# A planned two-layer transformer kernel: a port that one engine holds, loads in source order, and work that gets its engine in the plan

## The chip, the core and the metric

The program runs on one core of one Trainium2 chip. The core's engines each take their instructions in program order: TensorE (PE; its weight loads are shown apart as PEld), VectorE (DVE), ScalarE (ACT), GpSimd (POOL) and SyncE (SP), whose queue issues all DMA transfers here. The metric is the device time of one execution in microseconds, the median of several runs.

## The reference, cut to what matters

```python
for i in range(DEPTH):                      # DEPTH 2
    mod_lat = silu(c) @ ada_w[i] + ada_b[i] # six vectors: shift, scale, gate, twice
    mod_ctx = silu(c_ctx) @ ada_w[i] + ada_b[i]
    u_lat = modulate(rms_norm(h_lat, g_mix[i]), sh1, sc1)      # 512 x 1024
    u_ctx = modulate(rms_norm(h_ctx, g_mix[i]), csh1, csc1)    # 256 x 1024
    if i == 0:   # 16 heads of 64; q, k normed per head; 8 x 16 neighbourhood plus all context, with a bias table
        y_lat = neighborhood_attention(ql, kl, vl, kc, vc, na_rpb) @ na_wo
        y_ctx = context_attention(qc, kc, vc) @ na_wo
    else:        # 16 query heads, 4 key heads, rotary; window of 128 plus all context, sink logits
        y_lat = sliding_window_attention(ql, kl, vl, kc, vc, sink) @ swa_wo
    h_lat = h_lat + ga1 * y_lat
    h_lat = h_lat + ga2 * (relu(modulate(rms_norm(h_lat, g_mlp[i]), sh2, sc2) @ w1) ** 2 @ w2)   # width 4096
    # in layer 0 the same for h_ctx
return h_lat
```

Everything is fp32. The kernel keeps that precision by splitting an operand x into a high part H (a cast on ACT to a format that TensorE reads fast) and a low part L = x - H (a subtraction), and by three products H·H, H·L and L·H.

## The kernel before, in words

The program has two layers, each with an attention and an MLP; in the order of time: the opening, the first attention (16 heads in 8 pairs), its output product, the first MLP, the second attention, its output product, the second MLP.

*The opening.* `ada01(q)`, q from 0 to 3, multiplies a quarter of the columns for the first layer's shift and scale with the conditioning vector (tile `s`): eight loads of `ada_w` each; `mods01(q)` transposes the result. `stats` sums squares of the input (`xT`, later `cT`); `mod0` makes from both the operands of the first products; `load0(p, units)` loads and splits a unit of `wqkv` for head pair p; `qkv0(0)` makes the 144 products (128 x 384) of pair 0. `bias_tables` copies 32 pieces of the position bias inside DRAM (tiles `bias_i`, `bias_e`); the heads load them from there.

*The attentions.* For each token tile `front` copies the product from PSUM, norms per head (`head_norm`, small operations on the tile `smalls`) and writes the result twice (`dup_mult`); `back` transposes it. `attn0` and `Head1` make scores, subtract the maximum, take Exp on ACT with its sum, a reciprocal on DVE, and normalise P with it, then transpose P (in layer 0 the first with the matrix `perm`) and multiply by V. In the layer-1 head, P has four tiles, two of 512 columns and two of 640.

*The MLPs.* `Stream` loads 128 x 1024 weight tiles and splits each (`split`); `relu2` makes the squared ReLU with one more subtraction `hL`. Beside the first MLP runs `ada(1, ...)`, the six vectors of layer 1 (48 tiles of `ada_w`): scalings on ACT and POOL and two additions of 128 x 1024 for nearly every tile on POOL.

*What sets the order.* Nothing is issued as the code runs. Each call makes a `Step` with an engine, and `Plan` records what it reads and writes. `Plan.search` then draws up an order for each engine: `forward` is a list scheduler which walks through time with a cost for every step (`cost`), takes the step of lowest rank that is ready, and models a port shared by DVE and POOL: a step with `port` waits until the port is free. The ranks come from latest start times (`latest`) and from gaps of TensorE (`hurry`), 40 rounds, the best one is kept. So all instructions carry the line of the call that issues them, L432. The engine of a step is written in the code, by `v`, `s`, `g`, `pe`, `sy`; for instance the subtraction in `split` is on `v` unless a caller asks for `g`.

## Time and profile before

| what | value |
|---|---|
| median of 3 runs | 1662.59 us (1661.06 to 1669.87) |
| the profiled execution, own time | 1661.9 us |
| its span, first to last instruction | 1660.1 us |
| TensorE busy | 1601.2 us, 96% |
| VectorE, ScalarE, GpSimd busy | 1136.5, 808.7, 553.9 us |
| moved by DMA | 165.63 MB, 100 GB/s over the span |
| mean granted TensorE clock | 0.992 of full speed |

Busy times are of the whole span; the stages differ, and the rows below are by stage. Idle time of an engine costs nothing unless TensorE or the last instruction waits for it. `FA`, `RA` and `R` are large SBUF tiles, each holding many things; `pq` are the eight PSUM banks.

### The profile page before, as it was taken

The numbers are of one execution on the slowest core, as the hardware profiler recorded it, in microseconds if no ns is written. First come the engines' busy times: TensorE is split into PE (matmuls) and PEld (weight loads), VectorE is DVE, ScalarE is ACT, GpSimd is POOL, SyncE is SP. The second block draws the span as 40 slices with busy tenths as digits, with TensorE's granted clock in tenths as the row PEclk, the third lists the DMA queues.
The fourth block names the chain that finished last, engine by engine and source line by source line (L and its number), as shares of the span: only waits on it lengthen the run. The fifth ranks groups of instructions, "written<-read, shape, count | busy, mean of one in ns | idle before, by whom it ended". The sixth has DMA issues, their size and how long they took to land.

```text
span 1660.1 us, 25159 instructions
## 1 busy us (share of the span) xinstructions
PE 1601.2 (96%) x9554; PEld 1357.5 (82%) x9554; DVE 1136.5 (68%) x2178; ACT 808.7 (49%) x1668; POOL 553.9 (33%) x371
## 2 busy tenths in 40 slices
PE   4999999999989999999999999999999899999999
PEld 3878888987778888888888888797767888888887
DVE  4787666778458656675666666899996766655654
ACT  4587666778435334344352433658874522332320
POOL 1121111122247419485682652475631400000000
PEclk9999999999999999999999999999999899999999
DMA  9723443114314334334342332010114232233301
GB/s 295 213 74 102 134 150 121 47 42 126 103 63 128 97 101 132 103 114 127 115 140 76 115 106 73 32 58 14 46 45 146 89 102 90 89 101 102 102 26 52
DMA packets 63802, 165.63 MB, mean 100 GB/s; under 512 B 6848, under 2 KB 24640, under 8 KB 63552
## 3 DMA queue, kind: packets, MB, share of 16 engines
q1 hardware_dynamic: 63680, 164.02, 31.2%
q8 instruction: 75, 1.23, 0.3%
q14 instruction: 47, 0.39, 0.1%
HBM read 159.79 MB, written 7.34 MB: 101 GB/s over the span
## 4 chain that ended last, share of the span: by engine, by line
PE 80%; DVE 8%; ACT 5%; issue 3%; DMA 3%; POOL 1%; SPq 0%; POOLq 0%; DVEq 0%; ACTq 0%
PE pq L432 80%; DVE FA L432 3%; DVE RA L432 2%; ACT RA L432 2%; DVE smalls L432 1%; DMA FA<-in_ada_w_dram 1%; ACT FA L432 1%; ACT R L432 1%; DMA FA<-in_wqkv_dram 1%; POOL FA L432 0%; DVE R L432 0%; ACT smalls L432 0%; DMA R<-in_ada_w_dram 0%; SPq L432 0%; DMA FA<-in_wo_dram 0%
## 5 line engine op out<-in xcount | busy, mean ns | idle before, releaser
L432 PE MATMUL pq<-RA 128*128 128x512 f32 (+3 forms) x6784 | 1268.5, 342 | 13.1 <-DVE RA L432 5.4
L432 PEld LDWEIGHTS pq<-RA 128*128 128x128 f32 x6784 | 1083.1, 190 | 166.8 <-issue 16.6
L432 ACT CAST RA<-FA 128x1024 fp32r<-128x1024 f32 (+3 forms) x283 | 224.9, 812 | 370.7 <-PE pq L432 256.5
L432 DVE TENSOR_TENSOR RA<-FA,RA 128x1024 fp32r<-128x1024 f32 (+3 forms) x249 | 297.5, 1209 | 113.6 <-ACT RA L432 109.9
L432 DVE SCALAR_TENSOR_TENSOR FA<-pq,mods,FA 128x512 f32<-128x512 f32 (+1 forms) x413 | 266.0, 662 | 138.6 <-PE pq L432 137.4
L432 POOL TENSOR_TENSOR R<-R,FA 128x1024 f32<-128x1024 f32 x84 | 218.2, 2628 | 6.7 <-ACT FA L432 4.6
L432 POOL TENSOR_TENSOR FA<-FA,smalls 128x512 f32<-128x512 f32 (+1 forms) x108 | 95.9, 892 | 322.5 <-DVE smalls L432 250.4
L432 PE MATMUL pq<-RA,R 128*128 128x512 f32 (+1 forms) x870 | 177.6, 353 | 3.4 <-DVE RA L432 3.4
L432 PEld LDWEIGHTS pq<-RA,R 128*128 128x128 f32 x870 | 144.4, 191 | 27.6 <-DVE RA L432 3.8
L432 POOL TENSOR_SCALAR FA<-FA,s 128x1024 f32<-128x1024 f32 x24 | 77.5, 3230 | 180.8 <-DMA FA<-in_ada_w_dram 166.0
L432 PE MATMUL pq<-ident,FA 128*128 128x128 f32 x802 | 124.1, 276 | 9.4 <-DVE FA L432 2.5
L432 PEld LDWEIGHTS pq<-ident,FA 128*128 128x128 f32 x802 | 92.0, 140 | 30.4 <-issue 9.4
L432 POOL TENSOR_TENSOR FA<-FA 128x256 f32<-128x256 f32 (+2 forms) x97 | 75.2, 791 | 120.2 <-ACT FA L432 109.4
L432 POOL TENSOR_TENSOR RA<-FA,RA 128x1024 fp32r<-128x1024 f32 (+2 forms) x34 | 72.4, 2140 | 128.5 <-ACT RA L432 96.4
L432 ACT COPY R<-pq 128x512 f32<-128x512 f32 (+3 forms) x200 | 89.6, 477 | 37.6 <-PE pq L432 36.4
L432 ACT ACTIVATE FA<-FA,smalls 128x512 f32<-128x512 f32 (+1 forms) x120 | 89.1, 743 | 25.4 <-DVE smalls L432 25.0
L432 ACT COPY FA<-pq 128x256 f32<-128x256 f32 (+4 forms) x130 | 56.1, 432 | 87.5 <-PE pq L432 80.1
L432 ACT ACTIVATE FA<-FA,s 128x1024 f32<-128x1024 f32 x60 | 69.1, 1151 | 60.1 <-POOL FA L432 50.8
L432 DVE SCALAR_TENSOR_TENSOR FA<-pq,FA 128x512 f32<-128x512 f32 (+1 forms) x96 | 57.1, 596 | 53.5 <-ACT FA L432 53.4
L432 ACT ACTIVATE FA<-pq 128x512 f32<-128x512 f32 (+1 forms) x96 | 49.9, 522 | 73.0 <-PE pq L432 71.9
L432 ACT ACTIVATE FA<-FA 128x256 f32<-128x256 f32 (+1 forms) x131 | 59.0, 457 | 49.5 <-DVE FA L432 38.3
L432 PE MATMUL pq<-R 128*64 128x512 f32 (+2 forms) x448 | 78.9, 463 | 0.0
(77 smaller groups left out, 979.1 us busy)
## 6 DMA issues: line engine op xcount, KB each, us to landing
FA<-in_w_dram SPq DMA_DIRECT2D x128, 512.0 KB, 3.5
FA<-in_ada_w_dram SPq DMA_DIRECT2D x80, 512.0 KB, 3.9
FA<-in_wqkv_dram SPq DMA_DIRECT2D x32, 384.0 KB, 3.7
FA<-in_wo_dram SPq DMA_DIRECT2D x16, 512.0 KB, 3.5
FA<-in_ada_w_dram SPq DMA_DIRECT2D x20, 256.0 KB, 5.9
FA<-in_wq_dram SPq DMA_DIRECT2D x8, 512.0 KB, 3.6
R<-in_ada_w_dram SPq DMA_DIRECT2D x12, 256.0 KB, 6.3
FA<-in_xT_dram SPq DMA_DIRECT2D x4, 512.0 KB, 7.7
```

What stands on the lines that cost most here:

```text
L432: tc.keep_in_program_order(getattr(e, f)(*map(real, args), **{k: real(x) for k, x in kw.items()}))
```

## The change

It has three parts. First, the model of the shared port: a step waits for it only where the other engine holds it, the holder keeps it to the end of its step, a DVE step may begin 138 ns earlier, and POOL doesn't choose a step with `port` while DVE holds the port. Second, the loads made by `load` up to the end of the opening (`strict`) are chained: each may be planned only after the load ahead of it in the source has been issued. Third, a step may have several forms, one for each engine that can do it: `gv` for POOL or DVE, `sv` for ACT or DVE, and `scaled` (the normalisation of P) for all three. `forward` puts such a step on the lists of all its engines; the first-named engine drops it where another would end it earlier by more than the slack of its rank, and another engine takes it where its own would be too late. The subtractions of all splits, the additions of squares, the broadcasts and the normalisations become `gv` or `scaled`.

```diff
     def split(H_, L_, x, eng=None):
 
         s.copy(H_, x)
-        (eng or v).tensor_tensor(out=L_, in0=x, in1=H_.bitcast(F32), op=ALU.subtract)
+        gv.tensor_tensor(out=L_, in0=x, in1=H_.bitcast(F32), op=ALU.subtract)
...
+    gv, sv = Engine("gpsimd", "vector"), Engine("scalar", "vector")
+
+    def scaled(out, x, by, flat):
+
+        y = Step("POOL")
+        y.forms = {"POOL": ("tensor_tensor", (), dict(out=out, in0=x, in1=by, op=ALU.mult)),
+                   "DVE": ("tensor_scalar", (), dict(out=out, in0=x, scalar1=flat, scalar2=None, op0=ALU.mult)),
+                   "ACT": ("activation", (out, x, AF.Copy), dict(scale=flat))}
...
-    load = sy.dma_start
+    strict = [True]
+
+    def load(out, in_):
+
+        x = sy.dma_start(out, in_)
+        if strict[0]:
+            if strict[1:]:
+                x.after = strict.pop().i
+                x.deps.add(x.after)
+            strict.append(x)
...
+            if e == "POOL" and owner == "DVE" and port > t and L[now[e][0][1]].costs[e][2]:
+
+                free[e] = port
+                continue
             k, i = heapq.heappop(now[e])
             x = L[i]
+            if x.forms:
+                own, slack = x.costs[e][1], k - t
+                if e == x.eng:
+                    best = min(max(free[o], t) + c[1] for o, c in x.costs.items())
+                    if free_choice and t + own > best + max(50.0, slack):
+                        dropped.add(i)
+                        continue
+                elif i not in dropped:
+                    main = max(free[x.eng], t) + x.costs[x.eng][1]
+                    if not free_choice or slack > main - t + 200 or main <= t + own:
+                        heapq.heappush(coming[e], (t + 300, k, i))
+                        continue
+                gone[i] = True
+                eng[i] = e
...
-                hold = max(0.0, port - t) if x.port else 0.0
-                free[e] = t + hold + x.occ
-                end[i] = t + hold + x.dur
-                if x.port:
-                    port = free[e]
+                occ, dur, shared = x.costs[e]
+                hold = max(0.0, port - t - (138 if e == "DVE" else 0)) if shared and owner != e else 0.0
+                free[e] = t + hold + occ
+                end[i] = t + hold + dur
+                if shared:
+                    port, owner = end[i], e
...
-            if t == 0:
-                g.tensor_tensor(out=P, in0=P, in1=sm.broadcast_to([128, 512]), op=ALU.mult)
-            else:
-                v.tensor_scalar(out=P, in0=P, scalar1=sm, scalar2=None, op0=ALU.mult)
+            scaled(P, P, sm.broadcast_to([128, 512]), sm)
...
     weave((qk, 6), (bias_tables(), 16))
+    strict[0] = False
```

The plan is drawn up anew with this, so the order of every engine changes. No computation is added or removed: TensorE has 9044 instructions in the built program before and after. DVE goes from 2180 to 1750, POOL from 376 to 796 and ACT from 1510 to 1520. Three places of the order follow; in the changed file the issuing line is L473.

The queue of SP in the opening, before, from its fourth entry on:

```order
L432 DMA FA<-in_xT_dram 128x1024
L432 DMA FA<-in_ada_w_dram 128x2x256
L432 DMA FA<-in_xT_dram 128x1024
L432 DMA cst<-in_cst_dram 128x290
L432 DMA FA<-in_ada_w_dram 128x2x256
L432 DMA FA<-in_cT_dram 128x2048
L432 DMA FA<-in_wqkv_dram 128x768
L432 DMA FA<-in_ada_w_dram 128x2x256 x3
L432 DMA FA<-in_wqkv_dram 128x768
L432 DMA R_114<-in_ada_w_dram 128x2x256 x4
L432 DMA bias_e<-in_rpb_dram 16x8x128 x7
L432 DMA bias_i<-in_rpb_i_dram 16x8x256
```

And of the change, from its sixth entry on (ahead of these stand four loads of xT, the constants and eight of ada_w with one unit of wqkv):

```order
L473 DMA FA<-in_ada_w_dram 128x2x256 x2
L473 DMA R_115<-in_ada_w_dram 128x2x256 x6
L473 DMA FA<-in_wqkv_dram 128x768
L473 DMA FA<-in_cT_dram 128x2048
L473 DMA R_115<-in_ada_w_dram 128x2x256 x2
L473 DMA FA<-in_ada_w_dram 128x2x256 x6
L473 DMA FA<-in_wqkv_dram 128x768
L473 DMA FA<-in_ada_w_dram 128x2x256 x4
L473 DMA R_115<-in_ada_w_dram 128x2x256 x4
L473 DMA FA<-in_wqkv_dram 128x768
L473 DMA bias_i<-in_rpb_i_dram 16x8x256
L473 DMA bias_e<-in_rpb_dram 16x8x128
```

All 32 loads of `ada_w` for the first products and pair 0's four units of wqkv now stand ahead of the first bias table; before, 14 of the bias loads stood among them, and cT was ahead of most of `ada_w`.

GpSimd in the first MLP, before (`R<-R,FA` is an addition of `ada`, `TENSOR_SCALAR` its scaling):

```order
L432 TENSOR_SCALAR FA<-FA,s_81 128x1024
L432 TENSOR_TENSOR R_4411<-R_4411,FA 128x1024 x4
L432 TENSOR_SCALAR FA<-FA,s_81 128x1024
L432 TENSOR_TENSOR R_4411<-R_4411,FA 128x1024 x4
L432 TENSOR_SCALAR FA<-FA,s_81 128x1024
L432 TENSOR_TENSOR R_4411<-R_4411,FA 128x1024 x2
```

And of the change, from the first scaling on:

```order
L473 TENSOR_SCALAR FA<-FA,s_81 128x1024
L473 TENSOR_TENSOR RA<-FA,RA 128x1024
L473 TENSOR_TENSOR RA<-FA,RA 128x512
L473 TENSOR_TENSOR RA<-FA,RA 128x256
L473 TENSOR_TENSOR R_4410<-R_4410,FA 128x1024 x2
L473 TENSOR_TENSOR RA<-FA,RA 128x1024
L473 TENSOR_TENSOR R_4410<-R_4410,FA 128x1024 x2
L473 TENSOR_SCALAR FA<-FA,s_81 128x1024
L473 TENSOR_TENSOR RA<-FA,RA 128x1024
```

The subtractions of the weight splits (`RA<-FA,RA` of 1024) and of the squared ReLU (512 and 256), on DVE before, stand between those of `ada`. DVE keeps none of them in this stage.

GpSimd late in the second attention, before (`FA<-FA,smalls` of 512 is a broadcast or a normalised P, the others without smalls belong to the rotary):

```order
L432 TENSOR_TENSOR FA<-FA 128x256
L432 TENSOR_TENSOR FA<-FA,smalls 128x512
L432 TENSOR_TENSOR FA<-FA 128x256
L432 TENSOR_TENSOR FA<-FA,smalls 128x512 x2
L432 TENSOR_TENSOR FA<-FA 128x8x16 x2
L432 TENSOR_TENSOR FA<-FA 128x256
```

And of the change:

```order
L473 TENSOR_TENSOR FA<-FA,smalls 128x512
L473 TENSOR_TENSOR R_8947<-R_8947,smalls 128x640
L473 TENSOR_TENSOR FA<-FA,smalls 128x640
L473 TENSOR_TENSOR FA<-FA,smalls 128x512
L473 TENSOR_TENSOR RA<-FA,RA 128x1024 x2
L473 TENSOR_TENSOR FA<-FA 128x256
L473 TENSOR_TENSOR RA<-FA,RA 128x512
```

All four normalisations of a head are now here, where one was; the three others were `TENSOR_SCALAR` on DVE, which had 96 of these in both layers and keeps 3.

## Rows read from the trace of the kernel before

**Rows 1.** The profile's page: span and busy time by engine.

```profile
span 1660.1 us, 25159 instructions
...
PE 1601.2 (96%) x9554; PEld 1357.5 (82%) x9554; DVE 1136.5 (68%) x2178; ACT 808.7 (49%) x1668; POOL 553.9 (33%) x371
```

**Rows 2.** Stretches of the whole program; times in us, instructions in brackets.

```profile
core 0: us, PE busy (x) PEld busy (x) DVE busy (x) ACT busy (x) POOL busy (x), PEclk, DMA share, GB/s
0.00:20.00 20.00, 0.94 (x20) 0.87 (x24) 5.70 (x20) 7.56 (x14) 0.70 (x6) 1.00 0.92 319
20.00:36.00 16.00, 11.91 (x138) 8.29 (x130) 10.46 (x18) 7.13 (x16) 3.89 (x2) 0.89 0.83 236
...
50.00:60.00 10.00, 8.21 (x64) 7.22 (x54) 6.81 (x14) 3.17 (x7) 1.79 (x7) 0.83 0.71 159
60.00:95.00 35.00, 30.91 (x193) 27.77 (x191) 30.63 (x97) 27.15 (x83) 6.67 (x10) 1.00 0.50 157
100.00:395.00 295.00, 290.22 (x2015) 251.31 (x2015) 209.43 (x649) 215.03 (x608) 56.19 (x68) 1.00 0.32 101
...
515.00:1035.00 520.00, 520.00 (x3003) 452.00 (x3002) 349.48 (x456) 201.52 (x271) 299.31 (x116) 1.00 0.35 109
1040.00:1095.00 55.00, 51.15 (x298) 43.03 (x297) 49.06 (x92) 32.45 (x69) 28.83 (x35) 1.00 0.10 29
1095.00:1165.00 70.00, 69.47 (x532) 58.50 (x531) 64.32 (x178) 50.91 (x132) 43.74 (x52) 1.00 0.10 32
1165.00:1310.00 145.00, 137.20 (x917) 106.72 (x915) 121.06 (x261) 96.69 (x209) 55.20 (x43) 0.99 0.25 81
```

**Rows 3.** Timeline of PE in the opening: start us, us, instructions.

```profile
29.62 4.79 PE L432 MATMUL pq<-RA 128*128 128x384 f32 x17 [0.72 <-ACT RA L432]
...
53.80 1.08 PE L432 MATMUL pq<-R,s 128*32 128x128 f32 x16
...
59.75 8.31 PE L432 MATMUL pq<-RA 128*128 128x384 f32 x47
...
94.69 0.38 PE L432 MATMUL pq<-perm,FA 128*128 128x128 f32 x2
```

**Rows 4.** Timeline of SP's queue in the opening.

```profile
20.27 5.17 SPq L432 DMA_DIRECT2D bias_e<-in_rpb_dram  x7
...
57.32 1.01 SPq L432 DMA_DIRECT2D FA<-in_wqkv_dram  x2
```

**Rows 5.** DMA from 8 to 20 us.

```profile
DMA packets 2731, 4.65 MB, mean 387 GB/s; under 512 B 202, under 2 KB 2183, under 8 KB 2603
```

**Rows 6.** DVE groups by form, 1165 to 1310 us: count, busy us, mean ns.

```profile
L432 DVE TENSOR_SCALAR FA<-FA,smalls 128x640 f32<-128x640 f32 x15 | 13.5, 928 | 0.0
...
L432 DVE TENSOR_SCALAR FA<-FA,smalls 128x512 f32<-128x512 f32 x10 | 8.6, 855 | 0.1
L432 DVE TENSOR_TENSOR RA<-FA,RA 128x1024 fp32r<-128x1024 f32 x6 | 8.5, 1416 | 0.0
```

**Rows 7.** POOL, tiles R and FA, 560 to 1040 us: ns min/median/max.

```profile
L432 POOL TENSOR_TENSOR R<-R,FA x71: 2385/2425/3422, 559.7 to 974.7; 128x1024 f32<-128x1024 f32 x71
L432 POOL TENSOR_SCALAR FA<-FA,s x20: 2848/3032/4889, 618.0 to 968.4; 128x1024 f32<-128x1024 f32 x20
```

**Rows 8.** POOL, normalisations (1095 to 1310 us), 512-wide subtractions (100 to 400 us).

```profile
L432 POOL TENSOR_TENSOR FA<-FA,smalls x28: 1036/1042/1288, 1109.8 to 1252.5; 128x512 f32<-128x512 f32 x28
...
L432 POOL TENSOR_TENSOR RA<-FA,RA x3: 1286/1298/1809, 371.6 to 375.3; 128x512 fp32r<-128x512 f32 x3
```

**Rows 9.** The page's groups: POOL's work for layer 1's adaLN.

```profile
L432 POOL TENSOR_TENSOR R<-R,FA 128x1024 f32<-128x1024 f32 x84 | 218.2, 2628 | 6.7 <-ACT FA L432 4.6
...
L432 POOL TENSOR_SCALAR FA<-FA,s 128x1024 f32<-128x1024 f32 x24 | 77.5, 3230 | 180.8 <-DMA FA<-in_ada_w_dram 166.0
```

**Rows 10.** DVE, small operations (1095 to 1310 us), subtractions (1400 to 1655 us).

```profile
L432 DVE SCALAR_TENSOR_TENSOR smalls<-smalls x27: 124/159/2355, 1095.0 to 1207.5; 128x4 f32<-128x4 f32 x27
...
L432 DVE TENSOR_TENSOR RA<-FA,RA x51: 691/1216/1226, 1406.6 to 1637.0; 128x1024 fp32r<-128x1024 f32 x29, 128x512 fp32r<-128x512 f32 x22
```

More of the change, by code (lines that the diff above doesn't have):

```diff
@@ L93, in __init__ @@
         self.eng, self.calls, self.reads, self.writes = eng, [], [], []
-        self.epoch, self.deps, self.succ = None, set(), []
+        self.forms, self.costs = {}, {}
+        self.epoch, self.deps, self.succ, self.after = None, set(), [], None
         self.occ = self.dur = 0.0
@@ new lines, in cost, with vector_cost @@
+            forms = x.forms or {x.eng: x.calls[0]}
+            x.costs = {e: self.vector_cost(x, e, *c) for e, c in forms.items()}
+            x.occ, x.dur, x.port = x.costs[x.eng]
+    def vector_cost(self, x, eng, f, args, kw):
+        port = False
+        data = [(y, *width(y)) for y in x.reads]
+        n = max(width(y)[0] for y in x.reads + x.writes)
+        here = [(y, m) for y, _, m in data if self.space(y) == "SBUF" and m > 8]
+        psum = any(self.space(y) == "PSUM" for y in x.reads)
+        if eng == "ACT":
+            two = f == "activation" and len(data) > 1
+            dur = (165 + 0.81 * n if psum else 195 + 0.83 * n) + (95 if two else 0) + (90 if kw.get("accum_out") is not None else 0)
+            if n <= 8:
+                dur = 297.0 if two else 205.0
+            occ = dur - 105
+        elif eng == "DVE":
+            dur = 148 + 1.045 * n
+            if len(data) > 2:
+                dur += 62
+            if n <= 16:
+                dur = 157.0
+            elif f == "tensor_scalar" and not psum:
+                dur = 225 + 0.51 * n
+            occ = dur - 82 + (82 if kw.get("accum_out") is not None else 0)
+            port = f not in ("tensor_reduce", "reciprocal", "memset") and not psum and (len(here) > 1 or f in ("tensor_scalar", "tensor_copy") or n <= 8)
+        else:
+            wide = any(m < k for _, k, m in data)
+            dur = 470 + 2.33 * n if f == "tensor_scalar" else 80 + 0.8 * n if f in ("memset", "affine_select") else 170 + (1.75 if wide else 2.2) * n
+            occ = dur - 45
+            port = f not in ("memset", "affine_select")
+        return occ, dur, port
@@ L287, in forward @@
             if not x.deps:
-                heapq.heappush(coming[x.eng], (0.0, rank[x.i], x.i))
-        for _ in range(n):
+                for e in x.forms or (x.eng,):
+                    heapq.heappush(coming[e], (0.0, rank[x.i], x.i))
+        left, owner, dropped = n, None, set()
+        while left:
             t, e = min((max(free[e], min(([free[e]] if now[e] else []) + ([coming[e][0][0]] if coming[e] else []))), k, e) for k, e in enumerate(self.ALL) if now[e] or coming[e])[::2]
@@ L361, in latest @@
             for j in x.succ:
[L362 removed]
+                v = min(v, late[j] - (1.0 if x.eng == L[j].eng == "PE" or L[j].after == i else self.lag(x.eng, L[j].eng) + d))
             if i in after:
@@ L392, in search @@
         for k in range(rounds):
-            start, end, order, last = self.forward(rank)
+            start, end, order, last = self.forward(rank, k > 0)
             if best is None or last < best[0]:
```

99 lines of the change are left out of this document (43 added, 56 removed).

## The prediction

> **What bounds the kernel now.** I read the page first, then a table of stretches, then the timeline of the opening. The page says TensorE: 1601.2 of 1660.1 us busy, VectorE 68%, GpSimd 33% [rows 1]. That share hides something, because a matmul that stands alone is counted with its whole pipeline, so I use the weight loads (PEld) as the gauge. In the first MLP, where TensorE never rests, they are busy 452.00 of 520.00 us, a share of 0.869 [rows 2]. A stretch's PEld time divided by 0.869 is about what the same work would take without a gap; the remainder is lost time, an estimate from these rows. For 0 to 20 us it is 19, for 20 to 36 us 6.5, for 50 to 60 us 1.7, for 60 to 95 us 3: about 30 us lost in the opening. The first attention (100 to 395) loses 295 - 289 = 6. The first MLP is the gauge and loses nothing by it. The second attention loses 5.5 (1040 to 1095), 2.7 (1095 to 1165) and 145 - 123 = 22 (1165 to 1310), 30 in all. So some 65 us can be had, nearly all of it in two places.
>
> The two are short of different things. In the opening the data are late: the first wide product runs at 29.62 us, the last adaLN product of the first layer's shift and scale at 53.80, and the last product of head pair 0 at about 66 (59.75 plus 36 of its row's 47 products at 8.31/47 = 0.177 us each) [rows 3]. From 8 to 20 us the DMA engines move 387 GB/s [rows 5]; over 20 to 36 us they move 236 and over 50 to 60 us 159, still 83% and 71% busy [rows 2]. Those are the stretches in which the queue sends the bias tables: seven issues from 20.27 us on take 5.17 us [rows 4], ahead of adaLN weights that the first products need. In the second attention VectorE is the short one: 49.06 of 55, 64.32 of 70 and 121.06 of 145 us, while GpSimd has 55.20 of 145 [rows 2].
>
> **The opening.** The new queue puts xT first, then per quarter the eight adaLN loads and a unit of wqkv, and the bias tables behind all of it. What pair 0 needs is 4 x 512 KB of xT, 32 x 256 KB of ada_w, 4 x 384 KB of wqkv, 1 MB of cT and 145 KB of constants: 13.3 MB. At the rates of before, 20 us move 0.319 x 20 = 6.4 MB and the other 6.9 MB at 387 GB/s take 17.8 us, so all has left the queue at 38 us, and the last adaLN product can run at about 39 instead of 53.8. Behind its transpose stand 66 wide products in the new order, 66 x 0.177 = 11.7 us: pair 0 ends at about 52 instead of 66, 14 us sooner. The four splits of wqkv go from POOL to DVE, about 1 us each on an engine that in 60 to 95 us is busy 30.63 of 35, so part is given back there: I take **-12 us**. The bounds are -3 (the fronts of pair 0 and 1 on DVE swallow most) and -18 (DVE, rid of broadcasts there, follows too). The bias tables cost nothing by this count: 32 issues at 5.17/7 = 0.74 us are through about 24 us after the loads, near 60, where they were through at 57.32 before [rows 4]. The first attention's first transposes of P came at 94.69 [rows 3] and should come near 77 to 80, so the cover shrinks from over 30 us to some 15; once it is gone each us of lateness is a us of the path.
>
> **Free engines, second attention.** The softmax normalisations and the splits leave VectorE. In 1165 to 1310 us the three costliest groups of those are 15 x 928, 10 x 855 and 6 x 1416 ns, 30.6 us [rows 6], so DVE has at most 90 of 121 us. On GpSimd a normalisation of 512 takes 1.04 us and a plain subtraction of 512 1.30 [rows 8], one of 1024 2.39 [rows 7]; of 640 there is no row: at least the 1.04, at most 640/512 of the 1.30, so 1.6; I take 1.3, the 1.04 row stretched, since it is the same operation. That adds 15 x 1.3 + 10 x 1.04 + 6 x 2.39 = 44 us: GpSimd goes from 55 to at least 99 of 145, more with the smaller groups. So the stretch is no longer set by DVE at 83% but shared: TensorE needs 123, ScalarE 97, GpSimd 100 to 120. The floor would be 123, so -22 at best; GpSimd in program order and the longer chain from reciprocal to transpose (four normalisations in a row, 4.7 us for a head) keep half or more of the gaps: I take -8. In 1040 to 1165 at most 8 us are lost; the same relief gives -2. Together **-10 us**, bounds 0 and -24.
>
> DVE's tiny operations there have a median of 159 ns and a longest of 2355 [rows 10], as long as a whole GpSimd operation of 1024 (2.39): they wait out the neighbour. The more GpSimd runs, the more often; the long DVE operations that used to wait as well (TENSOR_SCALAR above) are gone. I cost this at 0, and its range lies in the bounds above.
>
> **First attention.** Splits and normalisations move likewise, but only 6 us are lost there: **-2 us**, bounds 0 and -5.
>
> **First MLP.** All splits and the low halves of the squared ReLU move to GpSimd, which already carries adaLN of layer 1. By the new order, from the last operations ahead of the first adaLN product to the last split of the stage GpSimd has 24 scalings, 146 operations of 1024, 32 of 512 and 32 of 256. With the shortest or median times of undisturbed ones (2.85, 2.39, 1.30; 0.7 for 256 as a little over half of 512) [rows 7, 8] that is 68 + 349 + 42 + 22 = 481 us; at the means of before (3.23, 2.63) [rows 9] 525. The stage lasts 520. In between lies the reason for the lower price: the means of before hold single operations of up to 3422 and 4889 ns, which overlap DVE operations that read two SBUF tensors, and in this stage those are the very ones that leave DVE. So the cover is some 39 us of GpSimd time, TensorE stays full: **0**, bounds 0 and, if GpSimd does end last, +5 from the 525.
>
> **The second MLP** runs TensorE full with GpSimd idle before; the splits fit. 0.
>
> **The sum.** 1661.9 us (the profiled execution's own time) - 12 - 10 - 2 = 1637.9. The median of the three runs is 0.7 above that execution, so **1638 us**, a gain of 1.5%.
>
> **The rivals.** *Slower: GpSimd becomes the bound of the first MLP.* The scalings and additions of adaLN wait for ScalarE, which waits for them, and the weight splits stand in the same queue. At 525 us of work plus 35 us of such waits the stage ends 40 us later, and 1638 + 40 = 1678. It decides slower from the point where work and waits pass 520 + 33 us. For it: 1.22 us on DVE [rows 10] become 2.39 for 112 splits. Against it: GpSimd's times in this stage are close to their shortest in the median (2425 against 2385 [rows 7]). The Trainium skill (GPSIMD Engine Reference, 4.1 Engine selection) speaks against the change as a whole: element-wise work on a tile belongs on VectorE, GpSimd being about twice as slow for two inputs. This trace agrees on the ratio (2.39 to 1.22); whether it costs time hangs on the cover above. I give this rival 0.12.
>
> *Opening only.* The second attention gets a new bound in GpSimd at 120 us plus its waits for reciprocals, and its 145 us stay: 1662.6 - 12 = about 1650. 0.17.
>
> *Nothing moves.* The first products come sooner but the fronts on DVE and ScalarE and the late bias tables hold the first attention to its old start; the rest cancels: 1655 to 1668. 0.13.
>
> *Both in full.* -18 in the opening, -24 in the second attention, -3 in the first: 1617. 0.16.
>
> The forecast itself has 0.42. **The numbers.** 0.5% (8 us) is about what a measurement of this kernel can tell from no change. Faster by more is the forecast, the opening alone and both in full: 0.42 + 0.17 + 0.16 = 0.75; within it 0.13; slower 0.12. The range goes from 1612, a little beyond both in full, to 1664, which takes in the opening alone and most of the no-change case and leaves out the slower one.
>
> **What would show it.** In the profile after: no bias table issue before the last wqkv unit of pair 0; the last adaLN product of the opening (the `s` products of 128 columns) near 39 us and the first `perm` transposes under 82. DVE's total falls from 1136 to some 700 us and POOL's rises from 554 to over 1000. In the first MLP TensorE has no idle time and the mean of a 1024 operation on POOL is near 2.4 us. In the second attention PEld's share rises above 0.78. I am wrong if TensorE waits for POOL in the first MLP, if the first `perm` transposes stay near 94, or if the second attention is still 270 us long.

## The result, and the profile after

The changed kernel takes **1666.36 us** (median of 20 runs, 1664.06 to 1668.95) where the kernel before takes 1661.39 (20 runs, 1659.71 to 1669.87): a ratio of 1.0023 over all runs, with a 95% interval of 1.0014 to 1.0033 (the medians alone give 1.0030). That is within the 0.5% that the prediction called no change, and on the slow side of it; 1638 was forecast, with a range up to 1664. This is the page of the changed kernel, its first lines:

```profile
span 1666.7 us, 25457 instructions
...
PE 1608.3 (96%) x9554; PEld 1357.6 (81%) x9554; DVE 794.8 (48%) x1748; ACT 820.7 (49%) x1678; POOL 1112.4 (67%) x791
```

VectorE lost 342 us of work and GpSimd gained 559 [rows 1], not far from the forecast (VectorE to some 700, GpSimd over 1000). TensorE's timeline shows the earlier opening, and the one place in the first MLP where TensorE stops:

```profile
19.92 0.44 PE L473 MATMUL pq<-RA 128*128 128x384 f32 x1 [1.49 <-ACT RA L473]
...
43.57 0.65 PE L473 MATMUL pq<-R,s 128*32 128x128 f32 x16
...
44.80 13.10 PE L473 MATMUL pq<-RA 128*128 128x384 f32 x74
...
88.79 0.39 PE L473 MATMUL pq<-perm,FA 128*128 128x128 f32 x2
...
819.72 3.74 PE L473 MATMUL pq<-RA 128*128 128x512 f32 x21
830.14 2.07 PE L473 MATMUL pq<-RA 128*128 128x512 f32 x4 [6.68 <-DVE FA L473]
```

Against [rows 3] the first wide product comes 9.7 us sooner, the last adaLN product 10.2, pair 0's last wide product (the 67th of the row's 74: 44.80 + 66 x 0.177 = 56.5) some 10, the first `perm` transposes 5.9. The stretches, with the columns of [rows 2]:

```profile
20.00:36.00 16.00, 15.54 (x163) 12.27 (x163) 9.50 (x19) 6.92 (x16) 0.00 (x0) 0.89 1.08 366
...
515.00:1035.00 520.00, 513.21 (x2951) 445.48 (x2950) 197.02 (x334) 198.97 (x266) 470.66 (x236) 0.99 0.34 108
...
1095.00:1165.00 70.00, 65.45 (x471) 52.85 (x472) 48.92 (x134) 50.56 (x125) 61.02 (x67) 0.98 0.08 24
1165.00:1310.00 145.00, 137.57 (x924) 105.87 (x922) 80.05 (x195) 101.94 (x218) 114.56 (x97) 1.00 0.24 79
```

In the second attention VectorE has the room that was wanted (80 of 145 us, before 121), and TensorE is no better off: PEld's share is 105.87/145 = 0.73, where over 0.78 was to show the gain.

**Where the time went.** TensorE does the same work in every kernel here: 9554 matmul records with the same columns. So each point of one kernel's work has its counterpart in another's. I took the records in the order of their starts, weighted them with their columns, and for the share of the work that the kernel before had started at the time at the head of a column, noted how much later (+) or sooner (-) the other kernel had started as much, in us. Kernels of nearly the same order show how far one execution can be off: the changed kernel, e3_late_amod and the two variants of it below (e14_dummy, e15_plain) lie between -10.9 and -13.5 at 98 us.

```
                  98    400    505    800    838   1040   1105   1115   1200   1320
after          -10.9   -8.5  -11.5  -11.6   -3.3   -2.9   -1.8   +5.7   +7.1   +6.7
e1_opening      -8.3  -10.7  -11.6  -11.5  -11.5  -11.5   -9.9   -9.9   -8.6   -6.9
e2_engines      -3.7   -3.1   -7.4   -7.2   +2.0   +2.8   +2.9   +7.0   +8.3  +10.5
e3_late_amod   -13.3  -10.9  -14.5  -14.3  -14.3  -13.8  -12.3   -4.8   -3.3   -3.8
e4_port         -5.2   -1.8   -3.5   -3.5   -3.1   -1.8   +3.5   +8.8   +8.5  +13.7
e5_old_port     -9.6   -9.0  -12.4  -12.2   -2.7   -2.0   +1.6   +2.4   +3.4   +3.2
e6_old_port_l. -10.0   -9.7  -11.3  -11.4  -11.4  -10.7   -7.4   -6.6   -5.6   -5.8
e10_no_norm    -10.2   -8.2   -9.1   -9.0   -9.0   -8.8   -8.9   -6.9   -9.2  -12.7
e13_norm_dve   -13.7  -12.4  -15.4  -15.3  -15.3  -15.0  -13.2   -9.9  -10.1   -4.5
e17_no_clause  -12.7  -11.8  -14.0  -14.1  -14.1  -13.7  -11.9  -11.1   -9.0   -7.4
e18_bias_free   -9.7   -9.0  -10.7  -10.9  -10.9  -10.3  -11.5   -4.9   -1.5   +1.0
```

The first row is the result in short: 11 us gained in the opening and still there at 800 us; 8 lost at one blow between 800 and 838, in a stage that had been counted safe; 7.5 more lost between 1105 and 1115, early in the second attention.

### The profile page after: what moved, and what is told of

It reads as the page before. It is cut to its first block, busy times and chain, and to the rows that moved or that the text cites. A ratio compares the mean times of both kernels' runs of the same rounds, so it can differ in the third digit from the quotient of the medians.

```text
span 1666.7 us, 25457 instructions
## 1 busy us (share of the span) xinstructions
PE 1608.3 (96%) x9554; PEld 1357.6 (81%) x9554; DVE 794.8 (48%) x1748; ACT 820.7 (49%) x1678; POOL 1112.4 (67%) x791
## 4 chain that ended last, share of the span: by engine, by line
PE 81%; DVE 7%; ACT 5%; issue 2%; POOL 2%; DMA 2%; SPq 0%; POOLq 0%; ACTq 0%; DVEq 0%
PE pq L473 81%; DVE FA L473 3%; DVE RA L473 2%; ACT FA L473 2%; ACT RA L473 2%; POOL FA L473 1%; DMA FA<-in_wqkv_dram 1%; DVE smalls L473 1%; ACT R L473 1%; POOL RA L473 1%; DVE amod L473 1%; SPq L473 0%; DMA FA<-in_ada_w_dram 0%; DMA R<-in_ada_w_dram 0%; ACT smalls L473 0%
## 5 line engine op out<-in xcount | busy, mean ns | idle before, releaser
L473 PE MATMUL pq<-RA 128*128 128x512 f32 (+2 forms) x6784 | 1272.5, 343 | 25.5 <-DVE FA L473 6.7
L473 PEld LDWEIGHTS pq<-RA 128*128 128x128 f32 x6784 | 1082.6, 190 | 179.3 <-issue 16.6
L473 POOL TENSOR_TENSOR RA<-FA,RA 128x1024 fp32r<-128x1024 f32 (+3 forms) x275 | 488.5, 1805 | 236.6 <-ACT RA L473 210.8
L473 ACT CAST RA<-FA 128x1024 fp32r<-128x1024 f32 (+3 forms) x283 | 225.2, 812 | 297.3 <-PE pq L473 206.5
L473 DVE SCALAR_TENSOR_TENSOR FA<-pq,mods,FA 128x512 f32<-128x512 f32 (+1 forms) x413 | 268.6, 665 | 204.4 <-PE pq L473 203.3
L473 POOL TENSOR_TENSOR FA<-FA,smalls 128x512 f32<-128x512 f32 (+3 forms) x241 | 205.1, 873 | 177.9 <-DVE smalls L473 160.9
L473 DVE SCALAR_TENSOR_TENSOR FA<-pq,FA 128x512 f32<-128x512 f32 (+1 forms) x96 | 57.7, 602 | 369.4 <-ACT FA L473 369.2
L473 POOL TENSOR_TENSOR R<-R,FA 128x1024 f32<-128x1024 f32 x84 | 202.2, 2451 | 0.0
L473 PE MATMUL pq<-RA,R 128*128 128x512 f32 (+1 forms) x870 | 179.1, 351 | 3.4 <-DVE RA L473 3.2
L473 PEld LDWEIGHTS pq<-RA,R 128*128 128x128 f32 x870 | 144.6, 189 | 28.5 <-DVE RA L473 4.1
L473 PE MATMUL pq<-ident,FA 128*128 128x128 f32 x802 | 129.7, 279 | 9.4 <-POOL FA L473 2.9
L473 PEld LDWEIGHTS pq<-ident,FA 128*128 128x128 f32 x802 | 93.4, 141 | 36.3 <-issue 12.8
L473 ACT COPY R<-pq 128x512 f32<-128x512 f32 (+4 forms) x212 | 94.6, 483 | 45.3 <-PE pq L473 43.9
L473 ACT ACTIVATE FA<-FA,s 128x1024 f32<-128x1024 f32 x60 | 69.1, 1151 | 94.4 <-POOL FA L473 65.8
L473 ACT ACTIVATE FA<-FA,smalls 128x512 f32<-128x512 f32 (+1 forms) x121 | 89.7, 743 | 32.7 <-DVE smalls L473 30.9
L473 POOL TENSOR_TENSOR R<-FA,R 128x1024 fp32r<-128x1024 f32 x25 | 61.0, 2442 | 47.6 <-ACT R L473 47.6
L473 ACT ACTIVATE FA<-pq 128x512 f32<-128x512 f32 (+1 forms) x96 | 49.7, 520 | 86.3 <-PE pq L473 74.7
L473 ACT COPY FA<-pq 128x256 f32<-128x256 f32 (+4 forms) x127 | 54.9, 433 | 73.6 <-PE pq L473 67.1
L473 POOL TENSOR_TENSOR FA<-FA 128x256 f32<-128x256 f32 (+2 forms) x113 | 78.7, 714 | 13.7 <-ACT FA L473 10.8
L473 ACT ACTIVATE FA<-FA 128x256 f32<-128x256 f32 (+1 forms) x131 | 59.0, 456 | 48.0 <-DVE FA L473 32.0
L473 DVE SCALAR_TENSOR_TENSOR RA<-pq,cst,RA 64x128 fp32r<-64x128 f32 (+2 forms) x152 | 58.3, 384 | 45.6 <-ACT RA L473 43.5
L473 PE MATMUL pq<-R 128*64 128x512 f32 (+2 forms) x448 | 80.1, 467 | 0.0
```

Source lines behind the costliest of these rows:

```text
L473: tc.keep_in_program_order(getattr(e, f)(*map(real, args), **{k: real(x) for k, x in kw.items()}))
```

## The experiments

The medians of the kernel before beside them were 1660.3 to 1661.4 us. The intervals given with the ratios reach some 1.5 to 3 us to either side.

**One part alone.** e1_opening is the kernel before with the chain of loads and nothing else of the change; e2_engines is the changed kernel without the chain:

```
e1:  -    load = sy.dma_start
     +    strict = [True]   (load() as in the change, with x.after; strict[0] = False behind the bias tables)
e2:  -    strict = [True]
     +    strict = [False]
```

> The kernel before with one part of the change alone: the loads of the opening leave in source order; engines and port model as before. Theory A (the opening's gain is real and lasts; the loss lies in the free engines): at equal work TensorE is 11 us ahead at 97 us, as in the changed kernel, and since VectorE and GpSimd share the work as before nothing is given back later: 1661.4 - 11 = 1650, 1647 to 1654. Rival B (the early start is given back by itself, because the weights of the following head pairs come no sooner): 1657 to 1662.

> The changed kernel with the opening's loads left to the order of before: free engines and port model alone. Theory A: the 11 us of the opening are missing and the losses behind it stay (8 us in the first MLP, 10 in and around the second attention): 1666.4 + 11 = 1677, 1671 to 1680. Rival B (the losses come from the earlier opening, which lets work collide that did not before): 1659 to 1665.

e1_opening took 1655.06 us (0.9965 of before, 0.9953 to 0.9978), e2_engines 1672.33 (1.0068, 1.0056 to 1.0081). e1_opening lies between its two forecasts, e2_engines in the range of its first. The chain is worth 5.7 us without the rest and 6.0 with it (1672.33 - 1666.36), half of the 12 forecast; a third pair, below, gives 1.8. The losses stay without it, so they don't come from the earlier opening.

**The first MLP.** In the changed kernel one VectorE operation of 128x16 takes 8.87 us beside an unbroken run of GpSimd. VectorE's timeline there, and GpSimd's (with two rows of the second attention, for later):

```profile
820.07 0.24 DVE L473 TENSOR_TENSOR mods<-pq,cst 128x8 f32<-128x8 f32 x2 [3.77 <-ACT FA L473]
820.22 0.41 DVE L473 SCALAR_TENSOR_TENSOR FA<-pq,FA 128x256 f32<-128x256 f32 x1
820.55 8.87 DVE L473 SCALAR_TENSOR_TENSOR amod<-mods,cst 128x16 f32<-128x16 f32 x1
829.34 2.18 DVE L473 SCALAR_TENSOR_TENSOR FA<-pq,mods,FA 128x512 f32<-128x512 f32 x4
```

```profile
808.84 19.46 POOL L473 TENSOR_TENSOR RA<-FA,RA 128x1024 fp32r<-128x1024 f32 x12
828.22 2.90 POOL L473 TENSOR_SCALAR FA<-FA,s 128x1024 f32<-128x1024 f32 x1
...
1102.89 3.52 POOL L473 TENSOR_TENSOR FA<-FA 128x128 f32<-128x128 f32 x6
1106.88 4.46 POOL L473 TENSOR_TENSOR FA<-FA,smalls 128x640 f32<-128x640 f32 x4 [0.47 <-DVE smalls L473]
```

Behind the `amod` product stand the evacuations of the second product (`FA<-pq,mods,FA`); their PSUM banks fill up, and TensorE waits 6.68 us. It is its only wait of the stage. While it stands still the granted clock falls to 0.50 of full speed (1.2 GHz), and the first products behind the wait run at that.

```profile
830.00:832.00 2.00, 1.86 (x4) 1.49 (x5) 1.53 (x4) 0.84 (x1) 2.00 (x2) 0.50 0.53 207
832.00:834.00 2.00, 2.00 (x11) 1.75 (x10) 0.86 (x2) 0.31 (x1) 2.00 (x2) 0.72 0.00 0
```

From 830.14 to 834 us the clock costs 1.86 x 0.50 + 2 x 0.28 = 1.5 us, so 6.68 become some 8 (an estimate from these rows). `amod` there is the scale of the second MLP, which nobody needs for 500 us. e3_late_amod takes it out of `ada` and puts it behind the first MLP; in the traces two rows of VectorE's order and two of TensorE's change with it:

```
-            if kind in (1, 4):
+            if kind == 1:
...
+    x = v.scalar_tensor_tensor(out=amod[1][:, 1], in0=mods[1][:, 4], scalar=1.0, in1=gmlp[:, 1]...)
+    x.deps.add(x.i - 1)
```

> The changed kernel with one VectorE operation put elsewhere: the 128x16 product that makes the scale of the second MLP (amod, kind 4 of layer 1), which took 8.87 us at 820.55 beside GpSimd's unbroken run of operations, is done behind the first MLP, where its inputs are long ready and its result is not yet needed. Theory A (that one operation was held off the shared ports for four GpSimd operations, and the PSUM evacuations queued behind it stopped TensorE): the step of 8 us at 820 us vanishes, 1666.4 - 8 = 1658, 1656 to 1660. Rival B (GpSimd's run holds up whichever VectorE operation comes next, or TensorE would have stopped there for want of a GpSimd split): the loss stays within 2 us, 1664 to 1668.

It took 1658.35 us (0.9986, 0.9978 to 0.9995): 8.0 less, and the step at 820 is gone from its row of the table. VectorE's evacuations at the same place, in its timeline, no longer wait:

```profile
817.36 0.24 DVE L473 TENSOR_TENSOR mods<-pq,cst 128x8 f32<-128x8 f32 x2 [3.75 <-PE pq L473]
817.52 0.42 DVE L473 SCALAR_TENSOR_TENSOR FA<-pq,FA 128x256 f32<-128x256 f32 x1
817.99 1.20 DVE L473 SCALAR_TENSOR_TENSOR FA<-pq,mods,FA 128x512 f32<-128x512 f32 x2
```

They read one SBUF tensor beside PSUM, and take 1.20 us for two while GpSimd works without a pause. Is it the product or the place? e9_port_bench asks for VectorE's turn in the middle of seven GpSimd operations, 24 times:

> A bench that computes nothing of the model (its output is a sum of copies of x): 24 trials, in each GpSimd has seven operations of 128x1024 in a row (splits into fp32r in the first twelve trials, additions in the others) and VectorE, in the middle of them, does the two PSUM sums that write mods and then one operation with two SBUF inputs: the amod product 128x16 with an inner broadcast, the same without it, a product of 128x4, a subtraction of 128x512, each at three delays. Theory A (a held VectorE operation may lose at several boundaries, whatever it is): in some trials of every kind it waits past two or more GpSimd operations, over 4.9 us. Theory A2 (something about the amod product makes it lose, the others get in at the first boundary): the amod trials wait until the run's end, 7 to 14 us, the others at most 2.5 us. Rival (it never loses at a boundary; the 8.87 us had another cause): all at most 2.5 us.

The rows of the `amod` product in it (with a broadcast, without), and of the 512-wide subtraction; ns min/median/max:

```profile
L71 DVE SCALAR_TENSOR_TENSOR am<-mo,cst x6: 361/1294/2011, 19.4 to 256.3; 128x16 f32<-128x16 f32 x6
L72 DVE SCALAR_TENSOR_TENSOR am<-mo,cst x6: 440/1296/2019, 69.5 to 306.5; 128x16 f32<-128x16 f32 x6
...
L74 DVE TENSOR_TENSOR wide<-wide,res x6: 1074/1928/2649, 169.8 to 407.6; 128x512 f32<-128x512 f32 x6
```

None is passed over: the longest of these, 2.65 us, is no more than the rest of one GpSimd operation and its own time. So the bench did not bring the long wait about, and two kernels went back to its place, one with a different operation there, one with a plain second operand:

```
e14:  +            if kind == 4:
      +                v.tensor_tensor(out=dummy[:], in0=mods[layer][:, 4]..., in1=cst[:, 0:16], op=ALU.mult)
e15:  -    gg = (gmix if kind == 1 else gmlp)[:, layer].unsqueeze(2).broadcast_to([128, KT, 2])
      +    gg = gmix[:, layer].unsqueeze(2).broadcast_to([128, KT, 2]) if kind == 1 else gfull[:]
```

> The changed kernel with the late amod, and in the old place of the amod product another VectorE operation that nobody reads: a 128x16 product of mods and a constant, without a broadcast and without a third operand. Theory P (the place does it, GpSimd's run of operations with the next one always at hand): the dummy takes over 7 us and the time is near 1666. Theory O (the operation does it): the dummy takes at most 2.5 us and the time is near 1658.

> The changed kernel, with the amod product where it is, but its second operand a full 128x16 tile instead of a broadcast view of 128x8. Theory P (the place does it): 8 to 9 us again, 1666. Theory O (the broadcast operand does it): at most 2.5 us, 1658.

They took 1668.18 and 1665.66 us in their one run. VectorE's timeline in e14_dummy, and the row of the product in e15_plain:

```profile
818.94 8.37 DVE L473 TENSOR_TENSOR dummy<-mods,cst 128x16 f32<-128x16 f32 x1
827.23 2.18 DVE L473 SCALAR_TENSOR_TENSOR FA<-pq,mods,FA 128x512 f32<-128x512 f32 x4
```

```profile
L473 DVE SCALAR_TENSOR_TENSOR amod<-mods,gfull x1: 8384/8384/8384, 818.5 to 818.5; 128x16 f32<-128x16 f32 x1
```

A result that nobody reads is held as long as the product, and so is a product without the broadcast. So it is the place and not the operation, as far as three different operations can show it. The last suspect was the length of the run, since GpSimd had worked without a pause for 70 us by then:

> A bench that computes nothing of the model: 20 trials, in each GpSimd has 28 subtractions of 1024, 256 and 512 columns in a row, and VectorE asks with the amod product for two SBUF inputs after 3 to 31 us of them; in the second ten ScalarE casts beside it all the time. Theory R (a long run without a pause does it): the trials that ask late wait past several operations, over 3 us, those that ask early at most 2.5 us. Rival S (neither does): none over 2.6 us, and the condition stays open.

```profile
L88 DVE SCALAR_TENSOR_TENSOR am<-mo,cst x20: 186/957/2336, 20.9 to 974.0; 128x16 f32<-128x16 f32 x20
```

The longest wait is 2.34 us (e16_long_run, the product's row): a run of up to 31 us doesn't do it; 70 us were not tried. What lets GpSimd go on stays open.

**The planner's port model.** e4_port is the kernel before with the change's model of the shared ports (exclusive to an operation's end, and GpSimd's next operation undecided while VectorE owns them); e7_no_yield drops the second clause:

```
e7:  -            if e == "POOL" and owner == "DVE" and port > t and L[now[e][0][1]].costs[e][2]:
     -                free[e] = port
     -                continue
```

> The kernel before with only the planner's model of the shared ports replaced by that of the change (exclusive until the end of an operation, GpSimd held while VectorE owns it); opening and engines as before. Theory A (the model only reorders, and the losses come from the work moved to GpSimd): 1661, within 4 us either way, and no VectorE operation over 3 us. Rival B (the new order itself costs the time in the second attention): 1666 to 1672.

> The kernel before with the new port model but without its clause that keeps GpSimd's next operation undecided while VectorE holds the ports. Theory A (that clause pushes GpSimd's operations back in the order, and they are what the heads of the second attention wait for): most of the 15 us go, 1661 to 1665. Rival B (the longer hold, until an operation's end, does it): 1670 to 1677.

e4_port took 1675.58 us (1.0089, 1.0075 to 1.0103): with not one operation on another engine, the new order alone is 15 us slower, more than either forecast had. e7_no_yield took 1660.28 (0.9994, 0.9975 to 1.0013), though one held operation costs it 5 us (last section): the clause, not the longer hold, makes e4_port slow. How much of this is the luck of one order? e8_control is the kernel before with VectorE's fixed cost in the planner 151 instead of 148 ns; e11_port_control and e12_opening_151 do the same to e4_port and e1_opening.

> A control: the kernel before with VectorE's fixed cost in the planner 151 instead of 148 ns, which changes the order in hundreds of places and means nothing. Theory A (an order's price is a property of the model): within 3 us of 1661. Rival C (the plan is a local optimum, and any change of its numbers draws a new one worth up to 10 us either way, above all in the second attention): further than 4 us from 1661.

> The kernel before with the new port model (1675.6) and the meaningless change of the control, VectorE's fixed cost 151 instead of 148 ns. Theory A (the 15 us belong to the new model's clause): 1671 to 1680. Rival C (they are the luck of one draw of the order): below 1667.

> The loads in source order alone (1655.1), with the meaningless change of the control. If the effects add: 1655 - 3.7 = 1651. If the control's gain was the opening's already (its trace was 8 us ahead at 110 us with the old loads): 1653 to 1657.

They took 1657.75 (0.998, 0.9962 to 0.9998), 1672.46 (1.0071, 1.0055 to 1.0088) and 1655.91 us (0.9969, 0.9956 to 0.9983). The control falls between its two forecasts; the other two show what the first theory (e11_port_control) and the second (e12_opening_151) said. A number that means nothing is worth 0.9 to 3.7 us; the 12 to 15 of the clause are more than that. But the chain is worth only 1.8 us between e8_control and e12_opening_151 (1657.75 - 1655.91): much of what it gains, another draw of the order gains without it.

With the free engines the same question has a smaller answer. e5_old_port is the changed kernel with the old model, e6_old_port_late that and the late `amod`, e17_no_clause the late `amod` with the new model but for the clause:

> The changed kernel (opening in source order, free engines) with the planner's old model of the shared ports. Theory A, as it stands after the first four runs (port model alone made the kernel 15 us slower, all of it from 1000 us on; free engines as such win a little): the 11 us of the opening last, the second attention loses nothing, and only the chance remains that one VectorE operation of the first MLP stands beside an unbroken GpSimd run: 1648 to 1653 without such an event, 8 us more with it. Rival B (the work moved to GpSimd costs the second attention its 7 us under any order): 1662 to 1670.

> As the run with the old port model and free engines, and the amod product of the second MLP behind the first MLP. Theory A: 1648 to 1653, no VectorE operation of the first MLP over 3 us. If the other run shows no starved amod, the two are equal within 2 us. Rival B: 1662 to 1667, equal to the late amod under the new model plus the noise of the order.

> The changed kernel with the late amod (1658.4), with the port model but without its clause that keeps GpSimd's next operation undecided while VectorE holds the ports. If the clause costs what the old model saved (3 us) and no new hold falls anywhere: 1653 to 1657. If the clause only hurts where GpSimd has little to do: 1657 to 1660.

They took 1663.30 (1.0006, 0.9988 to 1.0024), 1655.22 (0.9957, 0.9940 to 0.9974) and 1655.05 us (0.9970, 0.9959 to 0.9981): the first two 2 us above what theory A allowed (with the held product, and without), the third as its first case said. e5 to e6 is the `amod` again, 8.1 us; after to e5, e3 to e6 and e3 to e17 are 3.1, 3.1 and 3.3. The place is the step between 1105 and 1115 in the table (some half of it is made up for elsewhere). GpSimd's timeline there in e17_no_clause, to be laid beside its last two rows of the changed kernel above:

```profile
1096.31 1.87 POOL L469 TENSOR_TENSOR FA<-FA 128x256 f32<-128x256 f32 x3
1098.13 4.47 POOL L469 TENSOR_TENSOR FA<-FA,smalls 128x512 f32<-128x512 f32 x4
```

The four normalisations of a head (`FA<-FA,smalls`) run at 1098.13 there and at 1106.88 in the changed kernel, behind six rotary operations; TensorE, out of independent products by 1109, waits for the transposes. Its longest wait there is not for them, but for a tiny VectorE operation that began beside a GpSimd subtraction of 1024 columns (1116.71, 2.34 us) and waited it out; these are VectorE's and TensorE's timelines in the changed kernel:

```profile
1116.81 2.27 DVE L473 SCALAR_TENSOR_TENSOR smalls<-smalls 128x4 f32<-128x4 f32 x1
```

```profile
1119.40 0.65 PE L473 MATMUL pq<-RA 128*128 128x128 f32 x3 [2.18 <-DVE smalls L473]
```

Behind it the granted clock is 0.84 from 1120 to 1130 us. The same wait of 2.2 us stands in e3_late_amod, e14_dummy and e15_plain, and neither in e6_old_port_late nor in e17_no_clause. All eight kernels with the clause lose 3.4 to 7.5 us in these 10 us, e4_port, e11_port_control and e13_norm_dve among them, which have three of the four normalisations on VectorE, so late ones on GpSimd can't be the reason there. Of the ten without it (the kernel before among them) nine lose 0 to 2.0, one 6.6 (e18_bias_free, which has a cause of its own, below).

**The second attention.** e10_no_norm leaves the normalisations out of e6_old_port_late; e13_norm_dve puts them back, in e3_late_amod, where the kernel before had them:

```
e10:  -   for t in (0, 3, 1, 2):
      -       scaled(P[t], P[t], sms[:, t : t + 1].broadcast_to(...), sms[:, t : t + 1])
e13:  -       scaled(...)
      +       if t == 3: g.tensor_tensor(out=P[t], ...)      (as before the change)
      +       else: v.tensor_scalar(out=P[t], ...)
```

> As the run with the old port model, free engines and the late amod (1655.2), with the 64 softmax normalisations of the second attention left out, so that the rows of P are not divided by their sums there. Theory A (the prediction's gauge was wrong: TensorE itself needs nearly all of the 145 us between 1165 and 1310, and relief of the other engines is worth little): 1652 to 1656. Rival B (the gauge was right, 22 us are lost there to the chain of VectorE and GpSimd, and the normalisations are a good part of that chain): 1635 to 1645.

> The changed kernel with the late amod (1658.4), and the softmax normalisations of the second attention back on the engines of before (three on VectorE, one on GpSimd). Theory A (the relief of VectorE was paid for by a longer chain from the reciprocal to the transposes, four normalisations in a row on GpSimd): 1652 to 1655, gained between 1170 and 1300 us. Rival B (neither matters, the chain has slack): 1656.5 to 1660.

e10_no_norm took 1648.88 us (0.9929, 0.9909 to 0.9949), 6.3 less than with them and between the two forecasts; e13_norm_dve took 1658.96 (0.9983, 0.9970 to 0.9996), no different from e3, as its rival B said. By the table its sameness is a sum: with the normalisations back it is 6.8 us ahead of e3_late_amod at 1200 us and 0.7 at 1320. Why it loses there what it gained was not followed up. These are the windows of 1165 to 1310 us, of e1_opening (engines of before), e6_old_port_late (free engines) and e10_no_norm:

```profile
1165.00:1310.00 145.00, 135.03 (x881) 105.18 (x880) 121.07 (x252) 94.08 (x199) 51.83 (x37) 0.96 0.26 86
```

```profile
1165.00:1310.00 145.00, 134.84 (x882) 103.90 (x881) 85.26 (x187) 98.20 (x208) 110.09 (x86) 0.98 0.27 86
```

```profile
1165.00:1310.00 145.00, 138.89 (x915) 109.38 (x914) 81.30 (x187) 100.95 (x212) 71.97 (x51) 0.98 0.26 86
```

From the first to the second VectorE falls by 36 us, GpSimd rises by 58, and TensorE does the same work (135.0 and 134.8). VectorE's 83% was not the bound of the stretch. TensorE's idle time is 10 us in both, and 6 in the third, where 64 operations are gone altogether and GpSimd has 72 us instead of 110: GpSimd's load held at most 4 of the 10.

**The rest of the opening.** A suspect for the other half were the two weight units that leave SP's queue at 69.67 us, behind the last bias table. They were taken for the last two of pair 1, which they are not. SP's timeline after:

```profile
38.81 0.35 SPq L473 DMA_DIRECT2D FA<-in_wqkv_dram  x1
...
51.38 0.51 SPq L473 DMA_DIRECT2D FA<-in_wqkv_dram  x1
...
52.83 0.37 SPq L473 DMA_DIRECT2D FA<-in_wqkv_dram  x1
...
69.67 1.01 SPq L473 DMA_DIRECT2D FA<-in_wqkv_dram  x2
```

The fifth to the eighth unit in the queue are pair 1's: they leave at 38.81, 47.14, 51.38 and 52.83 us, before the change at 57.32, 57.95, 64.19 and 64.66, so they come 12 us sooner. The two at 69.67 are pair 2's first, whose products begin at 108 us; before they left at 70.96.

e18_bias_free lets loads pass the tables (`if chain: strict[1:] = [x]`, with `chain=False` for the tables).

> The changed kernel with the late amod and without the port model's clause (1655.05), and in the opening the bias tables wait for the last load of head pair 0, but the loads behind them may pass them: the last two weight units of pair 1 leave the queue near 57 us instead of 70. Theory A (those two units were what ate half of the opening's gain): TensorE is 3 to 6 us further ahead at 98 us and the kernel 3 to 6 us faster, 1649 to 1652. Rival B (TensorE is held there by the fronts of pairs 0 and 1 on VectorE and ScalarE, not by weights): 1653.5 to 1657.

It took 1660.11 us (0.9989, 0.9978 to 1.0001), more than either forecast, and the two units did not move:

```profile
70.84 0.85 SPq L469 DMA_DIRECT2D FA<-in_wqkv_dram  x2
```

So what keeps the other half of the opening's gain stays open. The 5 us to e17_no_clause were lost elsewhere, by the table from 1105 us of the kernel before on. In the trace of e18_bias_free, whose execution took 1662.87 us, the place is a VectorE operation that waits past several GpSimd operations, once more, and again the clock falls behind TensorE's wait. VectorE's timeline, GpSimd's, TensorE's, and a window:

```profile
1095.20 3.99 DVE L469 SCALAR_TENSOR_TENSOR smalls<-smalls 128x4 f32<-128x4 f32 x1
```

```profile
1095.71 2.36 POOL L469 TENSOR_TENSOR RA<-FA,RA 128x1024 fp32r<-128x1024 f32 x1
1098.03 1.13 POOL L469 TENSOR_TENSOR FA<-FA 128x128 f32<-128x128 f32 x2
```

```profile
1099.91 6.67 PE L469 MATMUL pq<-RA 128*128 128x256 f32 x32 [3.29 <-DVE smalls L469]
```

```profile
1100.00:1105.00 5.00, 5.00 (x24) 5.00 (x25) 2.43 (x10) 2.74 (x7) 2.90 (x3) 0.50 0.16 66
```

The wait of 3.29 us and 5 us at half the clock (2.5 us) are 5.8 of the 6.6. Five of its twelve runs took 1656.8 to 1657.3 us, six 1661.3 to 1663.5; whether the operation is held in the slower ones alone, one trace can't show.

## Why the prediction was wrong

**The opening, -12: right in kind, half in size or less.** The mis-sized term is the chain's gain: with it and without it differ by 5.7, 6.0 and 1.8. The loads left the queue sooner than worked out (pair 0's last unit at 34.42 us, 38 forecast), but the last adaLN product came 10.2 us sooner instead of 14.8, pair 0 ended some 10 sooner instead of 14, and the first `perm` transposes came 5.9 sooner instead of 15. The bias tables, put at no cost, were through at 69.6 instead of near 60. The changed kernel does keep 11 us of lead to 800 us, so the forecast of 12 looks right there; that is in part luck, for some of this lead comes with the new order and not with the loads: e4_port and e8_control, without the chain, are 5.2 and some 7.5 ahead at 98 us too. What keeps the rest is open.

**The first MLP, 0: the step that failed.** Its throughput was forecast well: GpSimd was to carry 481 us of the 520, and it has 470.66; its additions have a median of 2447 ns:

```profile
L473 POOL TENSOR_TENSOR R<-R,FA x84: 2398/2447/2512, 514.8 to 973.0; 128x1024 f32<-128x1024 f32 x84
```

TensorE never waits for it, so the rival in which GpSimd becomes the bound fell. The rule of the Trainium skill that was weighed with it (GPSIMD Engine Reference, 4.1 Engine selection) holds in its ratio, 2447 ns to 1216 [rows 10], and did not decide the time. What failed is the sentence on VectorE's tiny operations: they "wait out the neighbour", as long as one GpSimd operation (2355 ns at most in [rows 10]), costed at 0. It was written for the second attention; in the first MLP, where GpSimd was to have hardly a pause, no such wait was priced at all, and the stage's only term was GpSimd's own time. One operation waited out the rest of one, four more and 1.1 us of a sixth, in a queue with PSUM evacuations behind it, and cost 8.0 us (8.1 in the second pair): 6.68 of waiting and the rest at the lower clock. What is queued behind the waiting operation on its engine was not asked. In the second attention too, the 0 was wrong: 2.18 us of TensorE's time went to one such operation. (Two slips that nothing rests on: of the 112 splits at 2.39 us that the rival names, the stage's trace has 59 of 1024 columns, and 1637.9 + 0.7 is 1638.6.)

**The second attention, -10: wrong.** The gauge promised more than could be had. PEld divided by 0.869 said 22 us lost in 1165 to 1310; for e10_no_norm it still says 145 - 109.38/0.869 = 19, when six of its 145 us are idle by the plain column. By the plain column 7.8 us were idle before [rows 2], and leaving all normalisations out brings 6.3. The plain column counts a lone product with its whole pipeline, so the truth may lie between; that a share taken from 512-column products doesn't carry over to a stage of transposes and 128-column ones is the likely reason, and was not measured. And the relief did not reach TensorE: 36 us less on VectorE left its 135 us as they were. That the chain of a head, which runs through as many operations on GpSimd as it did on VectorE, is what TensorE waits for fits this and the 6.3 us, and is argued. The free engines by themselves are worth nothing here: e6 and e17 against e1, 1655.22 and 1655.05 against 1655.06.

**The port model: no term at all.** The diff shows it and the order showed hundreds of moved rows; the prediction priced the moves of engine and the moves of loads, and not what a new order of the rest may cost. It is 3.1 to 3.3 us here (12 to 15 in a kernel with the old engines), near the 0.9 to 3.7 that a meaningless number moves. That the clause costs the step at 1105 us is likely (eight of eight lose there, and of ten without it only the one with a held operation), not proved; by which operations it does so differs from kernel to kernel.

**The sum as measured:** 1661.4 - 6 (chain) + 0 (engines) + 3 (port model) + 8 (the held product) = 1666.4; measured 1666.36. The terms are the steps over e1_opening, e17_no_clause and e3_late_amod to the changed kernel, so that they add up is no test. The 8.0 is far beyond the 0.9 to 3.7 of a meaningless number and has its place in the trace; the 3 is not. e1_opening, e6_old_port_late and e17_no_clause beat both kernels, by 0.3 to 0.43%, and agree within 0.2 us. With the late `amod` alone the change as made (e3_late_amod) is no longer slower than the kernel before.

## What to carry to other kernels

Before work goes to GpSimd, look at what VectorE still does with two SBUF inputs beside it, and at what stands behind that in VectorE's queue: an operation that nobody needs yet may not stand ahead of PSUM evacuations. Count a wait of TensorE as more than itself: in three places here some 1.5 to 2.5 us of lower clock came on top. A high busy share says what an engine does, not what the path waits for, so read the wait that ends last, and don't trust a gauge that comes from another stage's shapes before a run has tried it. Where a planner writes the order, run a meaningless change of its numbers as a control, since that alone moved this kernel by up to 3.7 us.

## What the runs showed of the hardware

An operation of VectorE with two SBUF inputs can be passed over. In ten of the traces I counted the ends of GpSimd operations at which such an operation (delayed by 0.5 us or more) stood waiting and GpSimd had its next one ready: at some 500 VectorE got in (522 by my count, 478 to 554 as the time allowed for "ready" is drawn). Six operations were passed over, three of them the product at 820 us, two for about 1 us, one in e7_no_yield, where VectorE's split waited for three additions and got in when they gave way to a scaling, as the product did (in the changed kernel 1.1 us into the scaling):

```profile
927.38 7.11 DVE L464 TENSOR_TENSOR RA<-FA,RA 128x512 fp32r<-128x512 f32 x1 [0.69 <-ACT RA L464]
```

```profile
924.39 9.54 POOL L464 TENSOR_TENSOR R<-R,FA 128x1024 f32<-128x1024 f32 x4
933.91 3.29 POOL L464 TENSOR_SCALAR FA<-FA,s 128x1024 f32<-128x1024 f32 x1
```

It cost that kernel 5 us, of which TensorE waited 3.31; the granted clock was 0.68 from 935 to 940. Later traces have more: the 3.99 us of e18_bias_free, and 4.94 us of a weight split in e12_opening_151 (702.54 us), which cost TensorE next to nothing (0.3 us by the table's reckoning). In e18_bias_free no scaling came: every GpSimd operation there is a `TENSOR_TENSOR`. The Trainium skill (SBUF — State Buffer, "SBUF: two separate sides") has the pair of ports as an exclusive lock, held for a whole instruction by whichever engine starts first. The traces agree on the lock, some 500 times; that a waiting VectorE operation may lose it several times in a row the page doesn't say, and 8.87 us beside operations of 2.4 us show it. The benches could not bring it about in 44 trials, so what decides it is open.
